# A copy and a transpose of the latest sums ahead of the ninth and fifteenth column block of every FFN

## The chip, the cores and the metric

The kernel runs on one core of a Trainium2 chip. The metric is the device time in microseconds of one execution of the whole program, as a median of several runs.

## The reference, cut to what matters

A decoder trunk of four layers for 256 tokens of width 1024, all in float32. Each layer has a token mixer (attention of three kinds: A, B, C, A) and a gated FFN with a short causal convolution, each between two RMS norms. The change lies in the FFN:

```python
D_MODEL, SEQ, DEPTH, D_FF, CONV_WIDTH = 1024, 256, 4, 2816, 3

def conv_ffn(h, w_up, conv_w, conv_b, w_down):
    S = h.shape[1]
    u = h @ w_up                                   # 256 x 5632: gate and value
    up = jnp.pad(u, ((0, 0), (CONV_WIDTH - 1, 0), (0, 0)))
    c = conv_b + up[:, CONV_WIDTH - 1:] * conv_w[CONV_WIDTH - 1]
    for j in range(CONV_WIDTH - 1):
        c = c + up[:, j:j + S] * conv_w[j]
    gate, val = jnp.split(c, 2, axis=-1)
    return (jax.nn.gelu(gate, approximate=True) * val) @ w_down

for i in range(DEPTH):
    g = norm_gains[i]
    h = h + rms_norm(mixer[i % 3](rms_norm(h, g[0])), g[1])
    h = h + rms_norm(conv_ffn(rms_norm(h, g[2]), ...), g[3])
```

## The kernel before, in words

**Weights.** All weights are packed into units of 128 x 1024 floats (512 KB). `next_unit` (L286) loads a unit into one of four buffers (`raw`) through SP's DMA queue and splits it in two parts for the matmuls: ScalarE copies it to the rounded type (`wh`, L278), and VectorE subtracts that from the original (`wl`, L279); in some mixers GpSimd does a share of the subtractions. There are six buffers each of `wh` and `wl`, so a split of unit n+6 waits until TensorE has read unit n. A product is made of three matmuls into the same sums (`mm3`, L318): high by high (L323), high by low (L324), low by high (L325).

**The FFN (`ffn`, L1378).** The gate and value columns are worked in 22 column blocks of 128 columns each (`NFF`). A block needs two units, one for its gate columns and one for its value columns. Its sums lie in one PSUM tile of 128 x 512: the gate's 256 tokens in the first half, the value's in the second (`ps[:, j * S : (j + 1) * S]`, L1408). One unit is 8 row blocks of 3 matmuls of 128 x 256, so a block is 48 matmuls. Blocks 0 to 2 are done by `early` together with the end of the norm; the loop at L1405 does blocks 3 to 21, with eight PSUM tiles in turn. `activate` (L1384) follows three blocks behind (`ACT_LAG`): ScalarE makes the first product of the convolution and its bias (`c`, L1389), VectorE adds two shifted products (L1392), ScalarE applies the GELU (`g`, L1396), VectorE multiplies gate and value (L1397), and `split` makes two parts of the result (`act`, L278 and L279). Behind the 22 blocks come the matmuls of the down projection (`y_ff`), which read `act` and 22 more units.

**What sets the order.** The program is recorded by a scheduler, which writes each engine's instructions in the order of its own simulated timeline; an engine then takes its queue in that order, and semaphores make it wait. `tc.issue_after(x)` keeps what is recorded inside it from being placed ahead of instruction x. `n_ffn`, the number of FFNs so far, and `halt` do not exist in this kernel.

**Other helpers that the steps speak of.** A transpose is a matmul of a 128 x 128 tile with the identity (`nc.tensor.transpose`, L482, L541, L565). Attention layers make logits (`s`, L965), turn them into weights on VectorE and ScalarE, transpose them (`pT`, L565) and multiply them with the values (`ot`, L559).

Of the kernel before, what the change touches and what calls it, by code (L numbers as in the profile page):

```python
# [10 lines left out]
F32 = mybir.dt.float32  # L11
F32R = mybir.dt.float32r
BF16 = mybir.dt.bfloat16
AF = mybir.ActivationFunctionType
# [5 lines left out]
P = 128  # L20
D = 1024
KB = D // P
S = 256
# [196 lines left out]
def halves(first, end):  # L220

    cut = max(first, end - 2)
    return [(k, h) for k in range(first, cut) for h in range(2)] + [(k, h) for h in range(2) for k in range(cut, end)]
# [3 lines left out]
class Trunk:  # L227
# [256 lines left out]
    def turn(self, more, n, after):  # L484

        nc = self.nc
        tok = self.work.tile([P, 512], F32, tag="z", bufs=2, name=f"tok{self.unit}")
        tok = tok[:, : 2 * n * P].rearrange("p (t n) -> p t n", t=2)
        nc.scalar.activation(tok, more.rearrange("p (t n) -> p t n", t=2)[:, :, : n * P], AF.Copy)
        out = self.ps_tr(f"turn{self.unit}")  # L490
        with ExitStack() as ctx:
            if after is not None:
                ctx.enter_context(self.tc.issue_after(after.ins))
            for t in range(2):
                for j in range(n):
                    nc.tensor.transpose(out[:, j * S + t * P : j * S + (t + 1) * P], tok[:, t, j * P : (j + 1) * P], self.ident)
        return out

    def rows_mm(self, y, xT, unit, half, start, stop):

        sl = slice(half * 512, half * 512 + 512)
        return self.mm3(y[half], xT, (unit[0][:, sl], unit[1][:, sl]), start, stop)
# [875 lines left out]
    def ffn(self, yT, L, finish, late):  # L1378
        nc = self.nc
        with self.tc.tile_pool(name="ffn", bufs=1) as fp:  # L1380
            cw = fp.tile([P, NFF, 2, 4], F32, name="cw")
            nc.sync.dma_start(cw, self.ins["conv"][L])
            act = [fp.tile([P, NFF, S], F32R, name=f"act{i}") for i in range(2)]
            def activate(i, ps):  # L1384
                c = fp.tile([P, 2, S], F32, tag="c", bufs=2, name=f"c{L}_{i}")
                for j in range(2):
                    u = ps[:, j * S : (j + 1) * S]
                    w = [cw[:, i, j, k : k + 1] for k in range(4)]
                    nc.scalar.activation(c[:, j], u, AF.Identity, bias=w[3], scale=w[2])  # L1389
                    for k in (1, 0):  # L1390
                        n = 2 - k
                        nc.vector.scalar_tensor_tensor(  # L1392
                            c[:, j, n:], in0=u[:, : S - n], scalar=w[k], in1=c[:, j, n:], op0=ALU.mult, op1=ALU.add
                        )
                g = fp.tile([P, S], F32, tag="g", bufs=2, name=f"g{L}_{i}")
                nc.scalar.activation(g, c[:, 0], AF.Gelu_apprx_tanh)  # L1396
                nc.vector.tensor_tensor(g, g, c[:, 1], op=ALU.mult)  # L1397
                self.split(act[0][:, i], act[1][:, i], g)

            tiles = [self.ps_mm(f"up{L}_{i}") for i in range(2)]  # L1400
            more = self.ps_one(f"up{L}_2")
            self.early(yT, [x[:, j * S : (j + 1) * S] for x in tiles for j in range(2)], late, more)
            self.prefetch(fp)
            behind = [(i, tiles[i]) for i in range(2)]
            for i in range(3, NFF):  # L1405
                ps = (self.ps_tr, self.ps_one, self.ps_ot, self.ps_ot, self.ps_mm, self.ps_mm, self.ps_tr, self.ps_tr)[i - 3 if i < 5 else 2 + (i - 5) % 6](f"up{L}_{i}")
                for j in range(2):
                    last = self.proj(ps[:, j * S : (j + 1) * S], yT, self.next_unit())  # L1408
                    if i == 3 and j == 0:
                        behind.append((2, self.turn(more, 2, last)))  # L1410
                behind.append((i, ps))
                while len(behind) > ACT_LAG:
                    activate(*behind.pop(0))
            for x in behind:
                activate(*x)
            y = [self.ps_y(t, f"ff{L}") for t in range(2)]

            def part(t, k, unit, half):
                x = [a[:, k, t * P : (t + 1) * P] for a in act]
                return self.rows_mm(y[t], x, unit, half, k == 0, k == NFF - 1)  # L1420

            for k in range(NFF - HOLD):
                unit = self.next_unit()
                for t in range(2):
                    for half in range(2):
                        part(t, k, unit, half)
            units = [self.next_unit((fp, XF) if k >= HOLD - XF else None) for k in range(HOLD)]
            for t in range(2):
                with ExitStack() as ctx:
                    if t == 1:  # L1430
                        ctx.enter_context(self.tc.issue_after(last.ins))
                    for k, half in halves(0, HOLD):
                        if t == 1 and k == HOLD - TAIL and half == 0 and self.turned:
                            ctx.enter_context(self.tc.issue_after(self.turned.ins))
                        last = part(t, NFF - HOLD + k, units[k], half)
                finish(t, y)


    def run(self):
        nc = self.nc  # L1440
        gain = self.setup()
        state = {}

        def enter(t, L, n):

            if t == 0:
                state["yT"] = self.new_yT(f"{L}_{n}")
            z = self.pre_norm(t, gains[L, n], f"pre{L}_{n}_{t}")
            if t == 0:
                self.transpose_in(0, z, state["yT"], f"{L}_{n}_0")  # L1450
            return z

        first = self.layers[0]
        gains = {(first, 0): gain}
        z = z_first = [enter(0, first, 0)]
        self.at_unit = {int(TUNED.get("E1", "3")): lambda: z_first.append(enter(1, first, 0))}
        g1 = int(TUNED.get("G1", "1"))
        if g1:
            self.behind.append((g1, [x.ins for x in self.yt_last], 1))
        name = f"{first}_0"  # L1460
        self.rows = None
        for n, L in enumerate(self.layers):
            for sub in range(2):
                yT, zs, was = state["yT"], z, name
                def late():
                    self.transpose_in(1, zs[1], yT, f"{was}_1")

                def prefetch(pool):
                    place = (pool, "gain", 2)
                    gains[L, 1 + 2 * sub] = self.gain(L, 1 + 2 * sub, place)  # L1470
                    if nxt:
                        gains[nxt] = self.gain(*nxt, place)

                self.prefetch = prefetch

                z = []
                last = n == len(self.layers) - 1 and sub == 1
                nxt = (L, 2) if sub == 0 else (self.layers[n + 1], 0) if not last else None

                def finish(t, y):  # L1480
                    self.post_norm(t, y[t], gains[L, 1 + 2 * sub], f"post{L}_{sub}_{t}")
                    self.turned = None
                    if nxt:
                        z.append(enter(t, *nxt))
                        if t == 0:
                            self.behind.append((self.unit + (4 if sub else 2), [x.ins for x in self.last], AHEAD))
                    else:
                        nc.sync.dma_start(self.out[0, t * P : (t + 1) * P], self.h[t])

                self.two_banks = sub == 0 and MIXER[L] == 0  # L1490
                with self.tc.tile_pool(name=f"psum{L}_{sub}", bufs=1, space=PSUM) as self.psum2:
                    if sub == 1:
                        self.ffn(yT, L, finish, late)
                    else:
                        (self.mixer_a, self.mixer_b, self.mixer_c)[MIXER[L]](yT, L, finish, late)
                if nxt:
                    name = f"{nxt[0]}_{nxt[1]}"
# [43 lines left out]
```

## Time and profile before

| what | value |
|---|---|
| runs | 1591.36, 1585.53, 1590.42 us (median 1590.42) |
| the profiled execution's own time | 1589.34 us |
| its span, first to last instruction | 1587.6 us |
| mean granted TensorE clock | 0.991 |
| busy: TensorE, VectorE, ScalarE, GpSimd | 1541.7, 1212.4, 978.3, 247.3 us |
| the four FFNs' blocks 3 to 21 start at | 319.1, 599.3, 943.4, 1412.5 us |
| DMA | 282.73 MB, mean 178 GB/s |

The time of an execution and its span differ by what lies around the first and the last instruction. Busy time is a union over an engine's instructions; matmuls overlap one another, so the row of a matmul group adds up to more than the engine's busy time, and the pace of TensorE is better read from the starts of successive matmuls in the timeline. The granted clock is the share of full speed that TensorE's clock gate let through.

### The profile page before, as it was taken

What the parts mean: (1) busy time and instruction counts of PE and PEld (TensorE: products, weight loads), DVE (VectorE), ACT (ScalarE), POOL (GpSimd) and SP (SyncE); (2) the same over time, 40 slices, a digit from 0 to 9 for tenths busy, and PEclk for the clock granted to TensorE, in tenths of its full rate; (3) what the DMA queues carried; (4) which work ended last, traced back from release to release, by engine and by line L of the source; (5) the groups of instructions that cost most, each with busy time, mean ns of one, the idle gap of its engine ahead of it and who ended that gap; (6) DMA issues with size and microseconds to landing.
All of it is one profiled execution on the core that took longest, in us unless ns stands there. A gap on an engine that the chain in (4) does not pass through costs nothing. (4 is left out here: it accounts for less than half of the span.)

```text
span 1587.6 us, 29208 instructions
## 1 busy us (share of the span) xinstructions
PE 1541.7 (97%) x11016; PEld 1436.6 (90%) x11016; DVE 1212.4 (76%) x2159; ACT 978.3 (62%) x1708; POOL 247.3 (16%) x312
## 2 busy tenths in 40 slices
PE   7999999999999899999997999999999999999998
PEld 6999999799988779998885789998999999889986
DVE  5687898798855768885688779876577889879863
ACT  5566666576644757664576667654566666667642
POOL 1433230000001510000113200000433332000000
PEclk9999999999999999999997999999999999999999
DMA  7665665565573556657563056566556665556562
GB/s 251 199 180 185 178 185 181 174 214 189 177 245 107 120 162 217 190 178 244 173 187 101 11 193 194 188 190 209 173 179 186 180 191 162 191 191 191 189 190 80
DMA packets 103724, 282.73 MB, mean 178 GB/s; under 512 B 10928, under 2 KB 40112, under 8 KB 103584
## 3 DMA queue, kind: packets, MB, share of 16 engines
q1 hardware_dynamic: 101376, 272.86, 55.3%
q0 software_dynamic: 2208, 8.01, 1.4%
q8 instruction: 87, 1.43, 0.4%
q14 instruction: 53, 0.43, 0.1%
HBM read 279.66 MB, written 1.16 MB: 177 GB/s over the span
## 5 line engine op out<-in xcount | busy, mean ns | idle before, releaser
L278 ACT ACTIVATE wh<-raw 128x1024 fp32r<-128x1024 f32 x443 | 466.0, 1058 | 350.4 <-PE up L324 122.8
L279 DVE TENSOR_TENSOR wl<-raw,wh 128x1024 fp32r<-128x1024 f32 x403 | 496.2, 1239 | 156.2 <-ACT wh L278 149.7
L324 PE MATMUL up<-yT,wh 128*128 128x256 f32 x1216 | 340.5, 280 | 0.0
L325 PE MATMUL up<-yT,wl 128*128 128x256 f32 x1216 | 339.8, 279 | 0.0
L323 PE MATMUL up<-yT,wh 128*128 128x256 f32 x1216 | 339.8, 279 | 0.0
L325 PEld LDWEIGHTS up<-yT,wl 128*128 128x128 f32 x1216 | 228.8, 188 | 0.0
L324 PEld LDWEIGHTS up<-yT,wh 128*128 128x128 f32 x1216 | 228.8, 188 | 0.0
L323 PEld LDWEIGHTS up<-yT,wh 128*128 128x128 f32 x1216 | 228.8, 188 | 0.0
L323 PE MATMUL qk<-yT,wh 128*128 128x256 f32 x768 | 216.6, 282 | 0.0
L324 PE MATMUL qk<-yT,wh 128*128 128x256 f32 x768 | 216.5, 282 | 0.0
L325 PE MATMUL qk<-yT,wl 128*128 128x256 f32 x768 | 216.4, 282 | 0.0
L1392 DVE SCALAR_TENSOR_TENSOR c<-up,cw,c 128x255 f32<-128x255 f32 x336 | 156.6, 478 | 5.1 <-ACT c L1389 2.5
L323 PEld LDWEIGHTS qk<-yT,wh 128*128 128x128 f32 x768 | 145.2, 189 | 2.3 <-issue 1.5
L324 PEld LDWEIGHTS qk<-yT,wh 128*128 128x128 f32 x768 | 145.3, 189 | 1.5 <-issue 0.7
L325 PEld LDWEIGHTS qk<-yT,wl 128*128 128x128 f32 x768 | 145.0, 189 | 1.5 <-issue 0.7
L323 PE MATMUL y_ff<-wh,act 128*128 128x512 f32 x352 | 138.2, 394 | 0.0
L325 PE MATMUL y_ff<-wh,act 128*128 128x512 f32 x352 | 138.1, 392 | 0.0
L324 PE MATMUL y_ff<-wl,act 128*128 128x512 f32 x352 | 136.9, 389 | 0.0
L384 POOL TENSOR_TENSOR r_post<-v_post,neg_half 128x1 f32<-128x1 f32 x16 | 8.8, 553 | 812.1 <-DVE v_post L382 812.1
L279 POOL TENSOR_TENSOR wl<-raw,wh 128x1024 fp32r<-128x1024 f32 x40 | 97.3, 2433 | 175.3 <-ACT wh L278 140.8
L324 PE MATMUL v<-wl,yT 128*128 128x256 f32 x400 | 113.8, 286 | 1.1 <-DVE wl L279 1.1
L323 PE MATMUL v<-wh,yT 128*128 128x256 f32 x400 | 114.4, 288 | 0.3 <-ACT yT L440 0.2
(245 smaller groups left out, 3143.4 us busy)
## 6 DMA issues: line engine op xcount, KB each, us to landing
raw<-in_weights_dram SPq DMA_DIRECT2D x473, 512.0 KB, 4.3
bias<-rows SPq DMA_DIRECT2D x160, 128.0 KB, 3.6
gain<-in_norm_gains_dram POOLq DMA_DIRECT2D x15, 512.0 KB, 4.9
out_dram<-h SPq DMA_DIRECT2D x2, 512.0 KB, 2.6
h<-in_x_dram SPq DMA_DIRECT2D x2, 256.0 KB, 3.3
gain<-in_norm_gains_dram SPq DMA_DIRECT2D x1, 512.0 KB, 6.2
h<-in_x_dram SPq DMA_DIRECT2D x1, 512.0 KB, 11.0
onehot<-in_onehot_dram SPq DMA_DIRECT2D x1, 448.0 KB, 12.6
```

What stands on the lines that cost most here:

```text
L278: self.nc.scalar.activation(hi, src, AF.Copy)
L279: return (engine or self.nc.vector).tensor_tensor(lo, src, hi.bitcast(F32), op=ALU.subtract)
L323: mm(out, lh, rh, start=start, stop=False)
L324: mm(out, lh, rl, start=False, stop=False)
L325: return mm(out, ll, rh, start=False, stop=stop)
L384: self.p_last = nc.gpsimd.tensor_tensor(r, v, self.neg_half, op=ALU.pow)
L1392: nc.vector.scalar_tensor_tensor(c[:, j, n:], in0=u[:, : S - n], scalar=w[k], in1=c[:, j, n:], op0=ALU.mult, op1=ALU.add)
```

## The change

In each FFN, ahead of blocks 8 and 14, a new helper `halt` copies 128 columns of the value sums of the block just finished out of PSUM, into a work tile that the norms use, and TensorE transposes that copy into the PSUM tile of the block that comes next. The block's own matmuls then overwrite it, so the result is unchanged. The kind goes by the FFN's number: FFN 0 copies on ScalarE and transposes once, FFN 1 copies on VectorE and transposes once, FFN 2 copies on ScalarE and transposes three times, FFN 3 copies on VectorE and transposes three times. The matmuls of blocks 8, 9, 14 and 15 may not be placed ahead of the last of these transposes.

```diff
+    def halt(self, ps, before, after, kind):
+
+        nc = self.nc
+        x = self.work.tile([P, D], F32, tag="z", bufs=2, name=f"halt{self.unit}")[:, :P]
+        if kind % 2 == 0:
+            nc.scalar.activation(x, before[:, S : S + P], AF.Copy)
+        else:
+            nc.vector.tensor_copy(x, before[:, S : S + P])
+        for n in range(1 if kind < 2 else 3):
+            last = nc.tensor.transpose(ps[:, :P], x, self.ident)
+        return last
...
+                if i in (8, 14):
+                    stop = self.halt(ps, behind[-1][1], last, self.n_ffn % 4)
                 for j in range(2):
-                    last = self.proj(ps[:, j * S : (j + 1) * S], yT, self.next_unit())
+                    with ExitStack() as ctx:
+                        if i in (8, 9, 14, 15):
+                            ctx.enter_context(self.tc.issue_after(stop.ins))
+                        last = self.proj(ps[:, j * S : (j + 1) * S], yT, self.next_unit())
                     if i == 3 and j == 0:
                         behind.append((2, self.turn(more, 2, last)))
...
             for x in behind:
                 activate(*x)
+            self.n_ffn += 1
...
         gain = self.setup()
+        self.n_ffn = 0
```

The change adds eight copies and sixteen transposes, and it lets the scheduler move others. ScalarE's queue at the end of block 7 of FFN 0, before (the first number behind `wh` and `raw` is the unit, `c0_7` belongs to block 7 of FFN 0):

```order
L278 ACTIVATE wh100_4469<-raw100_4467 128x1024
L278 ACTIVATE act0_3779<-g0_4_4315 128x256
L1389 ACTIVATE c0_6_4454<-up0_6_4174,cw_3777 128x256
L278 ACTIVATE wh101_4499<-raw101_4497 128x1024
L278 ACTIVATE act0_3779<-g0_5_4388 128x256
L1389 ACTIVATE c0_7_4527<-up0_7_4247,cw_3777 128x256
L278 ACTIVATE wh102_4542<-raw102_4540 128x1024
```

and of the change:

```order
L278 ACTIVATE wh100_4472<-raw100_4470 128x1024
L278 ACTIVATE act0_3779<-g0_4_4315 128x256
L1401 ACTIVATE c0_6_4457<-up0_6_4174,cw_3777 128x256
L278 ACTIVATE wh101_4502<-raw101_4500 128x1024
L504 ACTIVATE halt96_4321<-up0_7_4247 128x128
L278 ACTIVATE act0_3779<-g0_5_4391 128x256
L1401 ACTIVATE c0_7_4530<-up0_7_4247,cw_3777 128x256
L1401 ACTIVATE c0_6_4457<-up0_6_4174,cw_3777 128x256
```

The copy has come in directly behind the split of unit 101; the split of unit 102 stands later than before. Block 14, and FFN 2, have the copy in the same place behind a split.

VectorE's queue at the end of block 7 of FFN 1, before:

```order
L279 TENSOR_TENSOR wl184_7615<-raw184_7612,wh184_7614 128x1024
L1397 TENSOR_TENSOR g1_5_7533<-g1_5_7533,c1_5_7526 128x256
L279 TENSOR_TENSOR act1_6925<-g1_4_7460,act0_6924 128x256
L1392 SCALAR_TENSOR_TENSOR c1_6_7599<-up1_6_7319,cw_6922,c1_6_7599 128x255
L279 TENSOR_TENSOR wl185_7645<-raw185_7642,wh185_7644 128x1024
```

and of the change, at block 7 and at block 13:

```order
L279 TENSOR_TENSOR wl184_7624<-raw184_7621,wh184_7623 128x1024
L1409 TENSOR_TENSOR g1_5_7542<-g1_5_7542,c1_5_7535 128x256
L279 TENSOR_TENSOR act1_6931<-g1_4_7466,act0_6930 128x256
L1404 SCALAR_TENSOR_TENSOR c1_6_7608<-up1_6_7325,cw_6928,c1_6_7608 128x255
L506 COPY halt180_7472<-up1_7_7398 128x128
L279 TENSOR_TENSOR wl185_7654<-raw185_7651,wh185_7653 128x1024
...
L279 TENSOR_TENSOR wl196_8065<-raw196_8062,wh196_8064 128x1024
L1404 SCALAR_TENSOR_TENSOR c1_12_8049<-up1_12_7766,cw_6928,c1_12_8049 128x255
L506 COPY halt192_7913<-up1_13_7839 128x128
L1404 SCALAR_TENSOR_TENSOR c1_12_8049<-up1_12_7766,cw_6928,c1_12_8049 128x254
```

The copy stands behind the first product of block 6, and the second time behind one of block 12. FFN 3 has it in the same places.

Away from the FFN, TensorE's queue in the attention of layer 2 has also moved (`s2_3` are the logits of head pair 3, `ot2_0_1` and `pT_2_1_0` values and transposes of pairs 0 and 1), before:

```order
L559 MATMUL ot2_0_1_9934<-pt0_0_9001,v_9192 128x256
L965 MATMUL s2_3_0_0_10085<-kd_9317,q_9016 128x256
L965 MATMUL s2_3_0_0_10085<-kl_9318,q_9016 128x256
L965 MATMUL s2_3_0_1_10086<-kd_9317,q_9016 128x512
L965 MATMUL s2_3_0_1_10086<-kl_9318,q_9016 128x512
L965 MATMUL s2_3_1_0_10110<-kd_9317,q_9016 128x256
L965 MATMUL s2_3_1_0_10110<-kl_9318,q_9016 128x256
L965 MATMUL s2_3_1_1_10111<-kd_9317,q_9016 128x512
L965 MATMUL s2_3_1_1_10111<-kl_9318,q_9016 128x512
L559 MATMUL ot2_0_1_9934<-pt0_1_9002,v_9192 128x256
```

and of the change:

```order
L571 MATMUL ot2_0_1_9946<-pt0_0_9013,v_9204 128x256
L977 MATMUL s2_3_0_0_10097<-kd_9329,q_9028 128x256
L977 MATMUL s2_3_0_0_10097<-kl_9330,q_9028 128x256
L571 MATMUL ot2_0_1_9946<-pt0_1_9014,v_9204 128x256
L571 MATMUL ot2_0_1_9946<-pt0_0_9013,v_9204 128x256
L571 MATMUL ot2_0_1_9946<-pt0_1_9014,v_9204 128x256
L571 MATMUL ot2_0_1_9946<-pt1_0_9015,v_9204 128x256
L577 MATMUL pT_2_1_0_0_10038<-ident_92,p1_2_1_0_9810 128x128
L577 MATMUL pT_2_1_0_0_10038<-ident_92,p0_2_1_0_9809 128x128
L577 MATMUL pT_2_1_0_0_10038<-ident_92,p1_2_1_0_9810 128x128
L977 MATMUL s2_3_0_1_10098<-kd_9329,q_9028 128x512
L977 MATMUL s2_3_0_1_10098<-kl_9330,q_9028 128x512
```

Six of the eight logit matmuls stand behind four value matmuls and three transposes now. SP's and GpSimd's queues hold the same work in the same order.

## Rows read from the trace of the kernel before

**Rows 1.** The page: busy us, share of the span and instructions of each engine.
```profile
PE 1541.7 (97%) x11016; PEld 1436.6 (90%) x11016; DVE 1212.4 (76%) x2159; ACT 978.3 (62%) x1708; POOL 247.3 (16%) x312
```

**Rows 2.** FFN 0, busy us: PE, PEld, DVE, ACT, POOL, PEclk, DMA, GB/s.
```profile
319.10:426.30 107.20, 107.20 (x921) 107.20 (x920) 96.50 (x163) 75.23 (x125) 0.00 (x0) 1.00 0.62 198
```

**Rows 3.** TensorE, FFN 0, starts of blocks 8 and 14: start, us, instruction.
```profile
347.80 0.28 PE L324 MATMUL up<-yT,wh 128*128 128x256 f32 x1
...
348.03 0.28 PE L323 MATMUL up<-yT,wh 128*128 128x256 f32 x1
...
381.63 0.28 PE L323 MATMUL up<-yT,wh 128*128 128x256 f32 x1
```

**Rows 4.** ScalarE, FFN 0, end of block 7: start, us, instruction, [idle before].
```profile
348.12 1.06 ACT L278 ACTIVATE wh<-raw 128x1024 fp32r<-128x1024 f32 x1 [0.98 <-PE up L324]
349.08 0.41 ACT L278 ACTIVATE act<-g 128x256 fp32r<-128x256 f32 x1
```

**Rows 5.** Instruction groups by shape: count | busy us, mean ns | idle before.
```profile
L1135 ACT ACTIVATE oT<-ot 128x256 fp32r<-128x256 f32 x8 | 3.1, 382 | 2.4 <-PE ot L325 2.4
L278 ACT ACTIVATE vhl<-cmp 128x64 fp32r<-128x64 f32 x1 | 0.2, 204 | 0.0
...
L1207 DVE COPY hidV<-hidT 128x128 f32<-128x128 f32 x2 | 0.5, 282 | 0.0
```

**Rows 6.** Waits of TensorE outside the FFN; the clock (columns of rows 2).
```profile
519.12 0.55 PE L1084 MATMUL pT<-ident,p 128*128 128x128 f32 x3 [1.72 <-POOL p L1078]
521.03 0.69 PE L1084 MATMUL pT<-ident,p 128*128 128x128 f32 x3 [1.36 <-POOL p L1078]
910.14 0.42 ACT L278 ACTIVATE oT<-o 128x256 fp32r<-128x256 f32 x1 [0.49 <-DVE o L581]
910.61 0.50 PE L323 MATMUL y_o<-wh,oT 128*128 128x512 f32 x1 [1.37 <-ACT oT L278]
...
520.00:525.00 5.00, 3.97 (x21) 3.98 (x22) 3.98 (x14) 3.67 (x11) 3.65 (x8) 0.66 0.67 159
909.00:914.00 5.00, 3.63 (x18) 2.83 (x17) 1.54 (x3) 1.95 (x5) 0.00 (x0) 1.00 0.00 0
```

**Rows 7.** TensorE, layer 0's attention: a stop, then transposes among matmuls.
```profile
82.71 0.44 PE L541 MATMUL pT<-ident,p 128*128 128x128 f32 x2 [0.47 <-DVE p L532]
82.90 0.36 PE L324 MATMUL qk<-yT,wh 128*128 128x256 f32 x1
83.11 0.87 PE L541 MATMUL pT<-ident,p 128*128 128x128 f32 x6
83.74 0.36 PE L325 MATMUL qk<-yT,wl 128*128 128x256 f32 x1
83.94 0.28 PE L323 MATMUL qk<-yT,wh 128*128 128x256 f32 x1
84.05 0.28 PE L324 MATMUL qk<-yT,wh 128*128 128x256 f32 x1
```

**Rows 8.** FFN 1, ends of blocks 7 and 13: TensorE's last matmul, VectorE.
```profile
628.09 0.28 PE L325 MATMUL up<-yT,wl 128*128 128x256 f32 x1
628.39 0.47 DVE L1392 SCALAR_TENSOR_TENSOR c<-up,cw,c 128x255 f32<-128x255 f32 x1
...
661.32 1.00 DVE L1392 SCALAR_TENSOR_TENSOR c<-up,cw,c 128x255 f32<-128x255 f32 x2
661.69 0.28 PE L325 MATMUL up<-yT,wl 128*128 128x256 f32 x1
```

**Rows 9.** Timeline of TensorE, layer 2's attention, behind the logits that moved.
```profile
853.66 1.05 PE L559 MATMUL ot<-pt,v 128*128 128x256 f32 x4
854.51 0.84 PE L565 MATMUL pT<-ident,p 128*128 128x128 f32 x3
...
857.22 0.36 PE L965 MATMUL s<-kd,q 128*128 128x256 f32 x1 [0.56 <-DVE nm L518]
859.42 0.75 PE L559 MATMUL ot<-pt,v 128*128 128x256 f32 x4 [0.81 <-DVE pt L279]
```

## The prediction, made before the changed kernel was run

> **What bounds the kernel now.** I read the page first. TensorE is busy 97% of the span, VectorE 76%, ScalarE 62% [rows 1], so the first question is whether TensorE has any slack where the change puts its waits. Next I read the busy time of each engine over the stretch in which an FFN works on its column blocks 3 to 21; one of the four stands in the rows, the others read alike. TensorE is busy 107.20 of 107.20 us at granted clock 1.00, its higher level (2.4 GHz), VectorE 96.50 and ScalarE 75.23 [rows 2]. Then I read the timelines at the place of the change. ScalarE stands idle 0.98 us until TensorE has read the buffer that the next weight split needs [rows 4], so the other engines run behind TensorE and not ahead of it. TensorE's pace: from 348.03 (first matmul of block 8) to 381.63 (first of block 14) are 6 blocks of 48 matmuls, 33.60 us, so 0.1167 us each, and the border of two blocks costs nothing (347.80 to 348.03 is two steps) [rows 3]. So here TensorE is the bound without a gap; what the change adds to its queue lengthens the run in full.
>
> **The change part by part.** Eight times, ahead of blocks 8 and 14 of each FFN, TensorE must drain, have 128 columns of its newest sums copied out, load the copy, transpose it, and start again. The transposes are overwritten, so nothing is removed to set against this. I price a wait up to the second matmul behind it, since the rows show a wider gap behind the first one.
>
> *The copy on ScalarE (FFN 0 and 2).* In the new order it stands directly behind the split of unit 101, and ScalarE takes its queue in order. That split starts at 348.12, 0.04 us after the L324 matmul that frees its buffer (347.80 + 0.28 = 348.08), and the instruction behind it at 349.08 [rows 3, 4]. So the copy starts at 349.08, though its sums, of a matmul at 347.92, are ready at 348.20. Its own time is in no row: ScalarE's copies out of PSUM take 382 ns for 256 columns and 204 for 64 [rows 5]; for 128 I take 0.27, near the straight line between them. It ends at 349.35. From the end of a ScalarE result to the matmul that waits for it the trace has 0.05 us (910.14 + 0.42 to 910.61) [rows 6], so the transpose starts at 349.40. How long from there to the block's first matmul? After a stop, two transposes stood ahead of the next matmul for 0.19 us (82.71 to 82.90), and six took 0.63 (83.11 to 83.74), 0.105 each [rows 7]. One transpose lies between 0 and 0.19: I take 0.10, the middle; three are 0.19 + 0.105 = 0.30. The matmul behind is followed after 0.20 us (83.74 to 83.94) [rows 7]. So the second matmul starts at 349.40 + 0.10 + 0.20 = 349.70 in place of 348.15 (348.03 + 0.117): 1.55 us with one transpose (FFN 0), 1.75 with three (FFN 2). By the order the copy ahead of block 14 stands behind a split in the same way, so 2 x 1.55 + 2 x 1.75 = **6.60 us**.
>
> *The copy on VectorE (FFN 1 and 3).* Ahead of block 8 it stands behind the first product of block 6, a scalar-tensor-tensor that starts at 628.39, when block 7 has just ended (628.09 + 0.28 = 628.37), and takes 0.47 [rows 8]. Instructions in a row start some 0.1 us before their forerunner's end (348.12 + 1.06 against 349.08 [rows 4]), so the copy starts at 628.76. A VectorE copy of 128x128 takes 282 ns [rows 5]: end 629.04, transpose 629.09, second matmul 629.39 in place of 628.32 (628.09 and two steps): 1.07 us, and 1.27 with three transposes. Ahead of block 14 the instruction before the copy starts at 661.32, long before the sums end (661.69 + 0.28 = 661.97) [rows 8], so the copy waits for TensorE alone: start 662.01 with the 0.04 of above, end 662.29, transpose 662.34, second matmul 662.64 in place of 661.92: 0.72, and 0.92 with three. Together 1.07 + 0.72 + 1.27 + 0.92 = **3.98 us**.
>
> *What queues behind the waits.* ScalarE spends 0.27 us on a copy where it has 0.98 idle ahead of each split [rows 4]; VectorE's copy falls into a time in which TensorE stands. The new order puts some splits a product or two later, but by that order VectorE has split unit 184 before TensorE starts on unit 180, four units of 24 matmuls or 2.8 us each ahead. I cost these at nothing; if that cover were gone, a late split would show as a wait of TensorE of up to the split's own 1.06 us [rows 4]. The transposes' target is the next block's own PSUM tile. No DMA is added, and SP's and GpSimd's queues keep their order.
>
> *The moved matmuls in layer 2's attention.* Six logit matmuls go behind four value matmuls and three transposes that stood at 853.66 to 855.35, so they come up to 1.7 us later; on the other side, the waits of 0.56 and 0.81 that follow could go away, 1.4 us [rows 9]. TensorE waits there for VectorE either way, so no row tells the sign. I take 0.
>
> *Sum.* 6.60 + 3.98 = 10.6 us. Bounds: copies between 0.20 and 0.38 us [rows 5] on both engines (-0.07 to +0.11, eight times), and the restart 0.1 either way, eight times: 9.2 to 12.3. The profiled execution took 1589.34 us, its span with what lies around it, so 1599.9 by this execution. The median of the three runs, 1590.42, is 1.1 above it: **1601.0 us**.
>
> One rule of the Trainium skill would make it dearer. The rows have 0.105 us for one more transpose in a row [rows 7]. The page "TensorE: Matmul & The Clock Gate", section "Part 4: PE-mode transpose", gives some 275 ns for a 128x128 transpose inside a kernel (for bf16; this one is fp32). By that figure, an estimate, the sixteen transposes would take 16 x 0.275 = 4.4 us where I have 4 x 0.10 + 4 x 0.30 = 1.6, and the change would cost 13.4, 1604. I go by the rows, because those transposes were issued in this kernel behind the same kind of wait.
>
> **The rivals.** *The clock falls.* A stopped TensorE may lose its granted clock. For it: after waits of 1.72 and 1.36 us close together, the granted clock of 520 to 525 was 0.66, so 3.4 us of the 5 were at the lower level (1.2 GHz) [rows 6]. Against it: a single wait of 1.37 us at 910.61 left it at 1.00 [rows 6]; my waits idle TensorE 1.20 us at most (348.20 to 349.40), and it is busy without a gap on both sides. Price: at half the clock, 3.4 us pass 1.7 us of work less; for the four ScalarE waits that is +6.8, 1608, for all eight +13.6, 1615.
>
> *It is partly given back.* While TensorE stands, the other two engines catch up, and a later wait of TensorE for them could shrink. Against it: inside the blocks TensorE has no such wait [rows 2]; those elsewhere begin at work that the pause delays as well. If half came back, 5.3 us remain: 1595.7.
>
> *Faster: the pause resets the pace.* 256 columns at 2.4 GHz are 0.1067 us, and TensorE takes 0.1167. If a drained queue restarted at the bare column rate, the blocks from 8 on (14 x 48 x 4 = 2688 matmuls) would gain up to 26.9 us; less the 10.6 spent that is 16.3 below today, 1574. It decides above 4.0 ns gained per matmul (10.6 / 2688). Against it: after the stop at 82.71 and its transposes, matmuls come at 83.94 and 84.05 [rows 7], which is the old pace.
>
> *It doesn't do what it says*, if the transposes were let through early: copy, transpose and matmul hang on one another through one tile, so I give this nothing.
>
> **How the numbers follow.** A measurement of this kernel can tell about 0.5% from no change, 8.0 us here: slower means over 1598.4. The forecast has 0.78; the runs of before lie 4.9 below to 0.9 above their median, and with the lower bound and the better case in layer 2 that puts 0.09 of it under 1598.4. The page's price has 0.05, the clock 0.05, giving back 0.09 (same), the faster pace 0.03. So slower 0.69 + 0.05 + 0.05 = 0.79, same 0.09 + 0.09 = 0.18, faster 0.03. The range goes down from 1601.0 by 1.4 for the lower bound, 1.4 for layer 2 and 2.7, half the spread of the runs, to 1595.5, which takes in half given back; up by 1.7 for the upper bound, 1.7 for layer 2 and 2.1 for the spread or a clock that falls once, to 1606.5.
>
> **What would show it.** In the changed profile: sixteen transposes that read `halt`; ahead of them TensorE idle about 1.20 us with ScalarE as releaser four times, and 0.72 and 0.37 us twice each with VectorE; ScalarE's copy beginning where a weight split ends; 0.1167 us a matmul and clock 1.00 between the waits; each FFN's blocks 3.1, 1.8, 3.5 and 2.2 us longer. Idle near 0.4 us ahead of ScalarE's transposes (the copy overtaking the split), a clock below 1.00 in the blocks, or a pace under 0.113 would prove me wrong.

## The result and the profile after

The changed kernel took 1602.35 us, median of 5 runs (1596.98 to 1604.89), against 1588.25 for 5 runs of the kernel before on the same chip (1585.53 to 1591.36). The two medians lie 14.1 us apart. The ratio on record, which is not the quotient of the medians, is 1.0062, with an interval of 1.0041 to 1.0083: 9.8 us slower (6.5 to 13.2). Why the two figures differ is not on record; runs of one kernel lie up to 6 us (before) and 8 us (changed) apart, so whole times show the effect but not its exact size. The forecast had 1601.0 and 10.6 us.

The page of the changed kernel, busy time by engine, beside [rows 1] (its execution took 1604.89 us):

```profile
PE 1546.1 (96%) x11032; PEld 1439.3 (90%) x11032; DVE 1214.9 (76%) x2163; ACT 979.9 (61%) x1712; POOL 249.2 (16%) x312
```

No engine has become another bound. What is new stands in the waits of TensorE (line and tile that waited, releaser: us in total, times, longest), where `halt` had no row before:

```profile
PE up L508 <- ACT halt L504: 4.8, 4, 1.2
...
PE up L508 <- DVE halt L506: 2.3, 4, 0.8
```

Four waits of 1.20 us for ScalarE, two of 0.76 and two of 0.39 for VectorE: 7.1 us of idle time. The durations of the new instructions, by the groups of the tile `halt`:

```profile
L508 PE MATMUL up<-ident,halt x16: 272/300/331, 354.1 to 1490.4; 128*128 128x128 f32 x16
L504 ACT ACTIVATE halt<-up x4: 258/259/260, 353.8 to 1018.6; 128x128 f32<-128x128 f32 x4
L506 DVE COPY halt<-up x4: 279/286/292, 635.1 to 1489.8; 128x128 f32<-128x128 f32 x4
```

The stretches in which the four FFNs work on blocks 3 to 21 (first the length and TensorE's busy time; behind all engines the granted clock), to be held against [rows 2]:

```profile
323.90:434.10 110.20, 107.80 (x923) 107.40 (x922) 96.87 (x163) 75.73 (x127) 0.00 (x0) 1.00 0.61 192
605.60:714.60 109.00, 107.85 (x924) 107.45 (x923) 97.07 (x165) 75.17 (x125) 0.00 (x0) 1.00 0.63 195
953.30:1064.00 110.70, 108.30 (x928) 107.90 (x927) 97.12 (x163) 75.74 (x127) 0.00 (x0) 1.00 0.62 192
1425.80:1535.20 109.40, 108.25 (x927) 107.86 (x926) 97.16 (x165) 75.43 (x125) 0.00 (x0) 1.00 0.63 194
```

From the start of the first matmul of block 3 to the start of the last one of block 21, each stretch took 107.18 us before. Now they take 110.25, 108.99, 110.68 and 109.41: longer by 3.07, 1.81, 3.50 and 2.23, together **10.61 us**. The clock is 1.00 in all four.

The profiled span grew by more, 1603.1 against 1587.6. Of those 15.5 us, 4.7 lie ahead of FFN 0, where the two kernels have the same work. There this one execution had a low clock once (0.66 over 10 us is 6.8 us at half, some 3.4 us of work), as the row of 20 to 30 us shows:

```profile
20.00:30.00 10.00, 7.98 (x40) 7.35 (x41) 4.72 (x6) 3.09 (x4) 0.00 (x0) 0.66 0.67 242
```

In another execution of the same kernel (e4 below) the clock from 15 to 30 us is 1.00, and FFN 0's blocks begin at 317.3 in place of 323.9. Layer 1's stretch gave 1.5 back and layer 2's took 1.7 more; both are taken up below. So stretches are compared one by one here, and whole times only over several runs.

One pause by ScalarE in the timeline (start, duration, engine, line), FFN 0, ahead of block 8; ScalarE first, then TensorE:

```profile
352.85 1.06 ACT L278 ACTIVATE wh<-raw 128x1024 fp32r<-128x1024 f32 x1 [0.98 <-PE up L324]
353.81 0.26 ACT L504 ACTIVATE halt<-up 128x128 f32<-128x128 f32 x1
...
352.65 0.27 PE L325 MATMUL up<-yT,wl 128*128 128x256 f32 x1
354.12 0.33 PE L508 MATMUL up<-ident,halt 128*128 128x128 f32 x1 [1.20 <-ACT halt L504]
354.21 0.36 PE L323 MATMUL up<-yT,wh 128*128 128x256 f32 x1
354.41 0.28 PE L324 MATMUL up<-yT,wh 128*128 128x256 f32 x1
```

The sums end at 352.92 (352.65 + 0.27), but the copy starts only as the weight split ends (353.81). Transpose 0.05 us after the copy, second matmul 0.29 us after the transpose's start. From the last matmul ahead to the second behind are 1.76 us, where two steps of 0.1167 stood: a cost of 1.53. The two kinds of pause by VectorE, FFN 1, ahead of block 8 and of block 14, each first VectorE and then TensorE:

```profile
634.67 0.47 DVE L1404 SCALAR_TENSOR_TENSOR c<-up,cw,c 128x255 f32<-128x255 f32 x1
635.07 0.28 DVE L506 COPY halt<-up 128x128 f32<-128x128 f32 x1
...
634.36 0.27 PE L325 MATMUL up<-yT,wl 128*128 128x256 f32 x1
635.40 0.33 PE L508 MATMUL up<-ident,halt 128*128 128x128 f32 x1 [0.76 <-DVE halt L506]
...
635.69 0.28 PE L324 MATMUL up<-yT,wh 128*128 128x256 f32 x1
...
669.37 0.29 DVE L506 COPY halt<-up 128x128 f32<-128x128 f32 x1 [0.20 <-PE up L325]
...
669.06 0.28 PE L325 MATMUL up<-yT,wl 128*128 128x256 f32 x1
669.72 0.33 PE L508 MATMUL up<-ident,halt 128*128 128x128 f32 x1 [0.39 <-DVE halt L506]
...
670.01 0.28 PE L324 MATMUL up<-yT,wh 128*128 128x256 f32 x1
```

Ahead of block 8 the copy begins behind another instruction of VectorE; ahead of block 14 VectorE is free and the copy waits for TensorE (`PE up L325`). Costs by the same reckoning: 1.10 and 0.72.

### The profile page after: what moved, and what is told of

It is laid out like the page before. It is cut to its first block, busy times and chain, and to the rows that moved or that the text cites. A ratio compares the mean times of both kernels' runs of the same rounds, so it can differ in the third digit from the quotient of the medians.

```text
span 1603.1 us, 29257 instructions
## 1 busy us (share of the span) xinstructions
PE 1546.1 (96%) x11032; PEld 1439.3 (90%) x11032; DVE 1214.9 (76%) x2163; ACT 979.9 (61%) x1712; POOL 249.2 (16%) x312
## 4 chain that ended last, share of the span: by engine, by line
PE 82%; DVE 6%; issue 5%; ACT 3%; POOL 2%; DMA 2%; SPq 0%; POOLq 0%; DVEq 0%; ACTq 0%
PE up L323 9%; PE up L324 9%; PE up L325 9%; PE qk L323 5%; PE qk L324 5%; PE qk L325 5%; PE y_ff L323 5%; PE y_ff L325 5%; PE y_ff L324 5%; PE s L977 3%; PE v L324 3%; PE v L323 3%; PE v L325 3%; DVE wl L279 2%; PE pT L553 2%
## 5 line engine op out<-in xcount | busy, mean ns | idle before, releaser
L325 PE MATMUL up<-yT,wl 128*128 128x256 f32 x1216 | 339.3, 279 | 0.0
L325 PEld LDWEIGHTS up<-yT,wl 128*128 128x128 f32 x1216 | 228.6, 188 | 0.0
L325 PE MATMUL qk<-yT,wl 128*128 128x256 f32 x768 | 216.1, 281 | 0.0
L1404 DVE SCALAR_TENSOR_TENSOR c<-up,cw,c 128x255 f32<-128x255 f32 (+1 forms) x336 | 157.2, 477 | 6.1 <-ACT c L1401 3.8
L325 PEld LDWEIGHTS qk<-yT,wl 128*128 128x128 f32 x768 | 144.9, 189 | 1.5 <-issue 0.7
L325 PE MATMUL y_ff<-wh,act 128*128 128x512 f32 x352 | 137.8, 392 | 0.0
```

Of the source, the lines that this page charges most:

```text
L325: return mm(out, ll, rh, start=False, stop=stop)
L1404: nc.vector.scalar_tensor_tensor(c[:, j, n:], in0=u[:, : S - n], scalar=w[k], in1=c[:, j, n:], op0=ALU.mult, op1=ALU.add)
```

## The experiments

The theory is that of the forecast: TensorE is the bound without slack, so a pause costs its own length in full. All edits are against the changed kernel. "Blocks" is the growth of the four stretches over 107.18.

### Transposes without a wait (e1)

```diff
-                    stop = self.halt(ps, behind[-1][1], last, self.n_ffn % 4)
+                    stop = self.halt(ps, behind[-3][1], last, self.n_ffn % 4)
```

> As the changed kernel, but the copy takes the sums of two blocks earlier (block 5 ahead of block 8, block 11 ahead of block 14), which are long complete, so TensorE has nothing to wait for; copies and transposes are all still there. Theory (the pauses cost the time that TensorE stands): idle ahead of the sixteen transposes under 0.1 us each; what is left is the transposes themselves, about 0.2 us for one and 0.4 for three with the wider gap behind, so blocks 3 to 21 of the four FFNs grow by 0.4, 0.4, 0.8, 0.8 us in place of 3.1, 1.8, 3.5, 2.2: 2.4 us in all, about 1591 when before reads 1588. Rival (the added instructions or the moved order cost it, not the wait): still 8 to 14 us over before.

Measured: ratio 1.0000 (0.9986 to 1.0013); blocks +0.24, +0.24, +0.67, +0.67, together 1.82 us. TensorE in the timeline of FFN 0:

```profile
346.21 0.28 PE L325 MATMUL up<-yT,wl 128*128 128x256 f32 x1
346.33 0.27 PE L508 MATMUL up<-ident,halt 128*128 128x128 f32 x1
346.36 0.36 PE L323 MATMUL up<-yT,wh 128*128 128x256 f32 x1
346.56 0.28 PE L324 MATMUL up<-yT,wh 128*128 128x256 f32 x1
```

No idle time in brackets, and the second matmul behind comes 0.35 us after the last ahead, 0.12 more than two steps. A single transpose costs 0.11 to 0.12 us and three cost 0.33 (0.67 / 2). Of the 10.6 us the transposes are thus 1.8, the waiting 8.8, of which 7.1 show as idle time. The expected 2.4 us were too much because the matmul behind starts 0.03 us after the transpose here, and not 0.10. TensorE's order in layer 2 is not that of the change in this run, so it tells nothing on the moved logits; e6 does.

### Twice as many pauses, only the next two blocks held (e2)

```diff
-                if i in (8, 14):
+                if i in (8, 11, 14, 17):
...
-                        if i in (8, 9, 14, 15):
+                        if i in (8, 9, 11, 12, 14, 15, 17, 18):
```

> The pause stands ahead of blocks 8, 11, 14 and 17 of each FFN, sixteen in place of eight. Theory (paid in full, nothing given back): blocks 3 to 21 of the four FFNs grow by twice as much, about 6.2, 3.6, 7.0 and 4.4 us, 21.2 in all; 1610 when before reads 1588, and the time outside the blocks does not shrink. Rival (partly given back, because the other engines catch up during a pause): the blocks still grow by 21 us but the whole by 15 or less. Rival (clock): a granted clock under 1.00 in the blocks and a growth of 1.7 us more for each place where it falls.

Measured: ratio 1.0080 (1.0061 to 1.0098); blocks +12.7 where 21.2 were expected, only 2.1 more than the change (1.8 for the added transposes). The new pauses ahead of blocks 11 and 17 have no idle time. TensorE ahead of block 11 in FFN 0, in the timeline:

```profile
369.16 0.28 PE L324 MATMUL up<-yT,wh 128*128 128x256 f32 x1
369.28 0.27 PE L508 MATMUL up<-ident,halt 128*128 128x128 f32 x1
```

and in the order of its queue (unit numbers behind `wh` and `wl`):

```
L324 MATMUL up0_10_4469<-yT1_0_2_3666,wh101_4502 128x256
...
L323 MATMUL up0_13_4691<-yT0_0_2_3665,wh107_4724 128x256
L324 MATMUL up0_13_4691<-yT1_0_2_3666,wh107_4724 128x256
L508 MATMUL up0_11_4542<-ident_92,halt102_4543 128x128
```

Block 13 was not held behind the transpose, and the scheduler filled the wait with it. The run added transposes, no waits, so it tells nothing on doubled waits. It suggests that a wait costs little where later blocks may pass it, which e10 puts to the test.

### No order held (e10)

```diff
-                        if i in (8, 9, 14, 15):
+                        if False:
```

> The same copies of the latest sums and the same transposes as in the changed kernel, but nothing holds the following blocks behind them: the scheduler puts some 30 matmuls of the next block (3.6 us) ahead of each transpose. Theory (it is the holding that costs): no idle ahead of the transposes, blocks grow by the transposes alone as with the old sums, 0.24, 0.24, 0.67 and 0.67 us, 1.8 in all; 1590 to 1591 when before reads 1589. Rival (the dependency on the latest sums costs wherever it stands): idle of 0.4 us or more ahead of the transposes, 1594 or more.

Measured: ratio 0.9996 (0.9981 to 1.0010); blocks +0.23, +0.62, +0.67 and +0.66, together 2.18, no idle ahead of any transpose. FFN 1's 0.62 in place of 0.24 comes from a slower pace behind its second transpose (last section). The same copies of the newest sums and the same transposes cost next to nothing if later blocks may pass them.

### Twice as many pauses, all later blocks held (e9)

```diff
-                if i in (8, 14):
+                if i in (8, 11, 14, 17):
...
-                        if i in (8, 9, 14, 15):
+                        if i >= 8:
```

> Four pauses per FFN again (blocks 8, 11, 14, 17), but now every block from 8 on is held behind the pause before it, so that the scheduler cannot put another block's matmuls into the wait, as it did at blocks 11 and 17 of the run before. Theory (paid in full): all sixteen pauses idle TensorE, 1.20 us on ScalarE and 0.4 to 0.8 on VectorE; blocks 3 to 21 grow by about 6.1, 3.6, 7.0 and 4.4 us, 21 in all, and the whole by as much, 1610 when before reads 1589. Rival (half given back in later waits): the blocks grow by 21, the whole by 11 or less.

Measured: ratio 1.0120 (1.0099 to 1.0141), which is 19.1 us (15.8 to 22.4); blocks +6.13, +3.25, +7.00, +4.13, together 20.5. The waits:

```profile
PE up L508 <- ACT halt L504: 9.6, 8, 1.2
PE up L508 <- DVE halt L506: 3.8, 8, 0.8
```

Eight times 1.20 for ScalarE, and 3.8 in eight for VectorE: two of 0.76 and six of 0.39, since the added VectorE pauses are all of the shorter kind. That is why twice the pauses cost a little under twice the 10.6. The growth inside the blocks shows up in the whole time. Giving back half (10.3) lies outside the interval.

### Half the pauses (e6, e7)

```diff
-                if i in (8, 14):
+                if i in (8, 14) and self.n_ffn < 2:
...
-                        if i in (8, 9, 14, 15):
+                        if i in (8, 9, 14, 15) and self.n_ffn < 2:
```

This is e6, with FFN 0 and 1 alone; e7 has `self.n_ffn > 1`, FFN 2 and 3 alone.

> The pauses of FFN 0 and 1 alone; the scheduler moves layer 2's logits as in the changed kernel. Theory: blocks of FFN 0 and 1 grow by 3.1 and 1.8 us, FFN 2 and 3 stay at 107.2: 4.9 in all, 1593 when before reads 1588. If the moved logits cost 1.8 us, layer 2's attention takes 238.7 us here too, and 1595; if that was chance, about 237 or either.

> The pauses of FFN 2 and 3 alone; layer 2's attention has the order of the kernel before. Theory: blocks of FFN 2 and 3 grow by 3.5 and 2.2 us, FFN 0 and 1 stay at 107.2: 5.7 in all, 1594 when before reads 1588. Layer 2's attention takes about 237 us if the moved order makes the difference, and may read 238.7 here as well if it was chance.

Measured: e6 1.0033 (1.0018 to 1.0048), blocks +3.07 and +1.81, the other two 107.18. e7 1.0032 (1.0021 to 1.0042), blocks +3.51 and +2.25. By the medians that is 5.3 and 5.5 us, for 4.9 and 5.8 in the blocks: the cost adds up by parts.

They also bear on the moved logits, since e6 keeps the new order in layer 2 and e7 has the old. The stretch between FFN 1's and FFN 2's blocks takes 237.0 (before), 236.8 (e3) and 237.5 (e7) with the old order, and 238.7 (the change), 239.3 (e4) and 234.6 (e6) with the new. Executions of one order differ by more than the two orders do. The whole time says more: with the new order e6 grew by 2.9 to 7.6 us (its interval) for 4.9 in the blocks, so the move costs between -2.0 and +2.7 us; whether it costs anything within that stays open.

### Both kernels once more (e3, e4)

> The kernel before, looked at once more, for how much the stretches outside the FFNs' blocks differ from one execution to the next. Theory (the difference between the two profiles outside the blocks, +4.7 us up to the first FFN's blocks, -1.5 in layer 1's attention, +1.8 in layer 2's, is chance): at least one of these stretches differs by 1.5 us or more from the first profile of this same kernel, while the blocks take 107.2 us each as before. Rival (the change made them): the stretches repeat within 0.3 us.

> The changed kernel, looked at once more. Theory: blocks 3 to 21 take 110.2, 109.0, 110.7 and 109.4 us again, within 0.1, while the stretch up to the first FFN's blocks is shorter than the 323.9 us of its first profile, where the clock was low for 6.8 us near the start; about 319 to 321. Layer 2's attention: within 0.3 us of 238.7 if the moved logits make it longer, nearer 237 if that was chance.

Measured: 1586.92 and 1600.35 us (one run each). All blocks of e3 take 107.18; those of e4 grow by 3.07, 1.81, 3.50 and 2.25, the change's own numbers within 0.02. Between the blocks, e4 has 173.0 us in layer 1 where the change had 171.5, and before has 173.0 where e3 has 171.4. So the 1.5 us of layer 1 come and go with the execution, not with the change. Two of e4's expectations missed: FFN 0's blocks begin at 317.3, earlier than 319 to 321, and layer 2 takes 239.3, neither the 238.7 of a fixed cost nor near 237.

### ScalarE's copy ahead of its split (e5)

ScalarE's copy is made to stand ahead of the weight split that it follows in the change; VectorE's copies stay. (The transpose's line becomes L509.)

```diff
-            nc.scalar.activation(x, before[:, S : S + P], AF.Copy)
+            copy = nc.scalar.activation(x, before[:, S : S + P], AF.Copy)
+            self.behind.append((self.unit + 5, [copy.ins], 1))
```

> As the changed kernel, but on ScalarE the split of the unit five ahead may not be placed ahead of the copy, so the copy stands in front of it in ScalarE's queue. Theory (0.85 us of each ScalarE pause is the place behind that split): idle ahead of the four ScalarE transposes falls from 1.20 to about 0.35 us; blocks of FFN 0 grow by 1.4 in place of 3.1 us, of FFN 2 by 1.8 in place of 3.5; FFN 1 and 3 stay at 1.8 and 2.2; 7.2 in all, 1595 when before reads 1588. Rival (ScalarE's copy is slow by itself, or the hand-over is): idle stays over 0.8 us. Rival (the split that comes 0.4 us later makes TensorE wait for weights): new waits of TensorE for wh or wl in blocks 8 to 14.

Measured: ratio 1.0036 (1.0022 to 1.0050), 5.7 us; blocks +1.40, +1.81, +1.82, +2.25, together 7.28. ScalarE and then TensorE in the timeline of FFN 0:

```profile
349.01 0.28 ACT L504 ACTIVATE halt<-up 128x128 f32<-128x128 f32 x1 [1.09 <-PE up L325]
349.18 1.05 ACT L278 ACTIVATE wh<-raw 128x1024 fp32r<-128x1024 f32 x1
...
349.34 0.33 PE L509 MATMUL up<-ident,halt 128*128 128x128 f32 x1 [0.37 <-ACT halt L504]
```

The copy now waits for TensorE, and TensorE's wait falls from 1.20 to 0.37 us, four times 0.83 = 3.3, as the blocks say (10.61 - 7.28). Over two thirds of each ScalarE wait was the place in ScalarE's queue, not the copy. The late split behind it cost TensorE nothing.

### Longer stops (e8, e11, e12)

e8 puts 1, 2, 4 or 6 (by FFN) further VectorE instructions on the copied tile ahead of a single transpose:

```diff
+        for n in range((1, 2, 4, 6)[kind]):
+            nc.vector.tensor_scalar(x, x, 1.0, None, op0=ALU.mult)
-        for n in range(1 if kind < 2 else 3):
+        for n in range(1):
```

> Longer pauses, to see when the granted clock falls: the copy is passed through 1, 2, 4 and 6 more VectorE operations (FFN 0 to 3) ahead of one transpose each, with other work of VectorE between them, so that TensorE stands some 2 to 6 us at a time. Theory (a single short wait between full work leaves the clock alone): the pauses of 2 us or less leave 1.00, as the 1.20 us ones do; the clock falls only behind the longer ones, and then the blocks grow by some 1.7 us more than TensorE stands, per fall. Rival (any stop can cost the clock): falls behind the 2 us pauses too. The blocks grow by the sum of the pauses otherwise.

Measured: 1636.9 us (one run). TensorE stood 2.52 us twice in FFN 0, 3.77 and 1.53 in FFN 1, and 4.17 to 7.0 after that. The last stop of FFN 0 and the 1.53 us stop of FFN 1, each followed by the window behind it, and a window around FFN 2's first stop (5.21 us, up to 995.09):

```profile
387.63 0.30 PE L510 MATMUL up<-ident,halt 128*128 128x128 f32 x1 [2.52 <-DVE halt L508]
...
388.00:393.00 5.00, 5.00 (x32) 5.00 (x31) 1.99 (x5) 1.65 (x3) 0.00 (x0) 0.66 0.36 111
...
676.72 0.30 PE L510 MATMUL up<-ident,halt 128*128 128x128 f32 x1 [1.53 <-DVE halt L508]
...
677.00:682.00 5.00, 5.00 (x46) 5.00 (x45) 4.22 (x8) 2.35 (x4) 0.00 (x0) 1.00 0.39 138
...
990.00:1000.00 10.00, 4.91 (x26) 4.94 (x27) 6.80 (x18) 4.35 (x10) 0.00 (x0) 0.66 0.36 106
```

At every stop of 2.52 us or more the clock fell to its lower level, and fewer matmuls were started; at 1.53 it did not. Behind the shorter of these stops it was low for 3.4 us (0.66 over 5 us); in FFN 2 and 3 it fell while TensorE still stood and was low for 6.8 us (0.66 over 10 us). The shortest stop with a fall is 2.52 us, the longest without one 1.53, and the change's longest is 1.20; no stop of around 2 us came about, so that part of the expectation is untested.

After FFN 0's second fall matmuls came slower than before even with the clock back at 1.00, up to the end of the blocks. e11 and e12 (the same kernel twice) ask what sets that pace: a long stop ahead of block 8, a transpose without a wait ahead of block 11, a wait of 1.20 us ahead of block 14.

```diff
-                if i in (8, 14):
-                    stop = self.halt(ps, behind[-1][1], last, self.n_ffn % 4)
+                if i in (8, 11, 14):
+                    stop = self.halt(ps, behind[-3 if i == 11 else -1][1], last, 0 if i > 8 else 4 + self.n_ffn)
...
-                        if i in (8, 9, 14, 15):
+                        if i >= 8:
```

with 1, 1, 3 and 3 further VectorE instructions ahead of block 8.

> On the pace behind a clock that fell and rose: a long pause (about 2.5 us and more) ahead of block 8 of each FFN, a transpose of long complete sums ahead of block 11 (no wait), a short wait on ScalarE ahead of block 14. Where the clock falls behind block 8's pause, the pace behind it may be over 0.1167 us a matmul, as it was 0.120 and 0.1178 behind two of seven falls in the run with longer pauses. Theory A (a drained queue starts at 0.1167 again): such a pace ends at block 14, with its wait. Theory B (any transpose does it): it ends at block 11. Theory C (neither; only another change of the clock does): it lasts to block 21.

> The same kernel once more, since only some of the falls leave another pace: the same expectations, on four more falls.

Measured: 1621.93 and 1625.67 us (one run each). The clock fell at block 8's stop (2.52 to 4.7 us) all eight times, and at block 14's 1.20 us never. The pace is read from the matmuls in 36 us at clock 1.00 (first count, which takes in the two or three that reach into the window from before it). e8, end of FFN 0:

```profile
395.00:431.00 36.00, 36.00 (x302) 36.00 (x301) 29.23 (x48) 22.89 (x37) 0.00 (x0) 1.00 0.61 182
```

e11, FFN 1 behind block 14:

```profile
680.00:716.00 36.00, 36.00 (x311) 36.00 (x310) 30.25 (x50) 22.93 (x37) 0.00 (x0) 1.00 0.61 180
```

e12, the same place:

```profile
681.00:717.00 36.00, 36.00 (x308) 36.00 (x307) 30.06 (x49) 22.62 (x37) 0.00 (x0) 1.00 0.58 180
```

and e10, FFN 1, where there was neither a wait nor a fall of the clock:

```profile
670.00:706.00 36.00, 36.00 (x308) 36.00 (x307) 31.37 (x52) 23.27 (x39) 0.00 (x0) 1.00 0.62 186
```

Counts of 311, 308 and 302 are spacings of 0.1167, 0.1178 and 0.120 us, by the starts of the matmuls. An interruption of the stream is mostly followed by 0.1167, in some places by 0.1178 and in one by 0.120, and the pace then holds until the next interruption. Of the eight falls only that of e11's FFN 1 left 0.1178, up to the transpose ahead of block 11, as theory B has it. But no theory held: in e11's FFN 2 the pace of 0.1178 began at that transpose, and in FFN 1 and 2 the wait ahead of block 14 was followed by 0.1167 in e11 and by 0.1178 in e12, with the same instructions. What chooses the pace stays open.

## Why the prediction was right

**What bounds.** TensorE without slack in the blocks: right. Doubling (e9), halving (e6, e7) and shortening (e5) the pauses each moved the blocks by the sum of the pauses' costs, and the whole time by the same within its interval.

**The copy on ScalarE.** Predicted 1.55 and 1.75 each, measured 1.53 and, with three transposes, 1.75 (half of 3.50); the idle time is 1.20 as forecast. The copy took 0.26 us where 0.27 was interpolated, and from the transpose to the second matmul 0.29 passed for 0.30. The step that carried the size, the copy's start at the end of the split, is shown by e5: with the copy ahead of the split the wait is 0.37.

**The copy on VectorE.** Predicted 1.07, 0.72, 1.27 and 0.92. FFN 1 has 1.10 and 0.72, FFN 3 together 2.23 where 2.19 was forecast. Idle times were 0.76 and 0.39 for 0.72 and 0.37: the copy behind the scalar-tensor-tensor began 0.03 us later than priced, at 635.07, that is 0.07 before its forerunner's end and not 0.1.

**The transposes.** Priced at 0.10 for one and 0.30 for three from [rows 7], measured 0.11 to 0.12 and 0.33 without a wait (e1). The Trainium skill, page "TensorE: Matmul & The Clock Gate", section "Part 4: PE-mode transpose", gives some 275 ns for a transpose inside a kernel. As time added to the stream, the way the forecast's 13.4 us takes it, the trace does not agree: sixteen cost 1.8 us in e1, and the blocks of the change grew by 10.6. As the duration of one transpose it fits: the rows of L508 have 0.27 in e1 and 272 to 331 ns in the change. But in e1 the matmul behind starts 0.03 us after the transpose (346.36 against 346.33), and what counts is the spacing.

**What queues behind, and layer 2.** Nothing late behind the copies: no new wait for `wh` or `wl` inside the blocks, not even in e5, which makes the split later. The 0 for the moved logits had no row behind it; e6 bounds it to -2.0 to +2.7 us, and within that it cannot be told from chance.

**The rivals.** The clock stayed at 1.00 in the blocks, and e8, e11 and e12 show that the clock does fall here at a single stop of 2.52 us or more, and not at 1.20 or 1.53. Giving back fell with e9. A pace quicker than 0.1167 appeared in no run, so the faster rival fell (the two starts that the forecast held against it, 83.94 and 84.05, are too few to tell 0.1167 from 0.1067); the paces that did appear besides it are slower. The transposes waited, so the change does what it says; e10 shows that this hangs on the held order.

**The sum.** 10.6 forecast, 10.61 in the blocks, 9.8 (6.5 to 13.2) by the ratio, 14.1 by the medians. The mechanism was right in each part, but an agreement to a few hundredths is luck: ScalarE's pauses with one transpose were priced 0.02 us too dear each, VectorE's behind the scalar-tensor-tensor 0.03 too cheap, and these cancelled in part; what the working could promise was its 9.2 to 12.3. That 1602.35 lies so near 1601.0 is luck too. The forecast counts from 1590.42, the median of three runs before; over five that median is 1588.25, and 10.6 on it makes 1598.9. One slip changes nothing: half the spread of the three runs is 2.9 us, not 2.7.

## What to carry to other kernels

Where a window of the trace shows the bounding engine busy without a gap, a wait put into its queue costs the time from its last instruction ahead to the second one behind, less what two instructions take without the wait, and in this kernel nothing that could be measured came back (e9); find out first whether later work may pass the waiting instruction, since then it may cost nearly nothing. Look for what stands ahead of the releasing instruction on its own engine: here a weight split in front of a 0.26 us copy made most of the wait. When single executions differ by almost as much as the effect, measure the stretch that was changed, and use the others to see how much comes by chance.

## What was not expected of the hardware

TensorE's pace on equal matmuls at granted clock 1.00 has more than one value: 0.1167, 0.1178 and 0.120 us, each kept until the next interruption; 0.120 appeared once, in e8, for some 40 us. It changed at stops and falls of the clock, but also at less: in e10 a transpose without a wait was enough. In the change itself all waits came back at 0.1167, so it plays no part in the 10.6 us; by an estimate from e8's spacing, 0.120 in place of 0.1167 cost 363 matmuls x 3.3 ns = 1.2 us behind FFN 0's second stop there.
